# Attention weights times v on one core: the first v in five transfers, cast by GpSimd instead of VectorE

## The chip, the core and the metric

The kernel runs on one core of a Trainium2 chip. The metric is the device time of one execution in microseconds (us), taken as the median of several runs; smaller is better. A profile of one more execution shows what each engine did and when: TensorE (PE, and PEld for its weight loads), VectorE (DVE), ScalarE (ACT), GpSimd (POOL), SyncE (SP) and the DMA engines.

## What is computed

For 8 x 12 = 96 heads, a 1024 x 1024 matrix of attention weights is multiplied by a 1024 x 64 matrix v, all in float32:

```python
def reference(attn_weights, v):   # (8, 12, 1024, 1024), (8, 12, 1024, 64)
    return np.einsum('bhqs,bhsd->bhqd', attn_weights, v).astype(np.float32)
```

The weights alone are 403 MB, so the kernel is for the most part one long stream of loads.

## The kernel before

The 96 heads are taken four at a time: 24 groups (`NV`), each cut into two units by its rows, so 48 units (`NU`). One partition of the tile holds the rows of one of 4 x 32 row blocks of the four heads. A unit's load brings [128, 16, 1024] weights from HBM into one of two buffers `abf` (unit n uses `abf[n % 2]`) and casts float32 to bfloat16 in the DMA itself: 4 MB written for 8 MB read. The program places every buffer and every semaphore by hand; each engine has its own written-out order, and only semaphores tie them together.

**PE** (lines 188 to 221) does, for each unit: wait for the unit's load; 16 groups g of 4 transposes (L132), which bring the summed dimension onto the partitions, into four PSUM banks in turn, so that group g must wait until group g - 4 has been copied out (L129); in the first unit of a group of heads, wait for v (`s_vr`, L197) and spread it over the partitions by small matmuls with a constant matrix (L147); transpose the previous unit's result back (L159); multiply, 64 matmuls (L174).

**VectorE and ScalarE** share the copies out of PSUM (L256 for the transposed weights: VectorE takes 10 of 16 groups, ScalarE 6), the spread v (L232), the products (L268) and the results (L239). VectorE's order starts with memsets (L303 to L307), then the wait for the first v and its cast (L308, L309), then the units.

**GpSimd** issues the loads. Its order is: loads of units 0 and 1 (L341, L342); five affine_selects that make the constants `ident` and `spread`; then for n = 0, 1, ... the load of unit n + 2 (L372, issued at L319), each behind a wait until VectorE's share of unit n's transposes is done on PE (L371), for that frees the buffer. In some rounds it also issues the load of a later v (L325) and the store of a finished result (L332). All of GpSimd's DMAs go through one queue to the 16 DMA engines.

**v**: the v of two groups of heads is loaded at a time. From the second pair on it comes by GpSimd's queue, cast to bfloat16 in the DMA. The first pair is loaded by SP's queue as float32 (L384 to L387) into `v32`, which is the memory of the last two slots of the output buffer, free at that time, and is cast by an engine into `vr`, a [128, 2, 8, 512] bfloat16 tile: 4096 elements a partition. The two halves of `v32` (index `two`) hold one group of heads each. The four transfers are pieces of (half, first partition, number of partitions), a row of 8 KB for each partition; each piece counts 16 on `s_v0`.

**SP** issues these four transfers first, then follows the loads: it tells PE when a unit's load is there (L393 to L396). In one unit (n = 33) it issues 15 tiny transfers of 1 to 15 rows into `small`, which nothing reads (L399 to L402). At the end it issues the last stores (L414 to L421).

The lines around the change: on VectorE, the last two of

```python
for h in range(2):
    nc.vector.memset(ot[:, :, ds(h * HP, HP)], 0.0).then_inc(s_ot[h])
nc.vector.wait_ge(s_v0, 16 * 4)
nc.vector.tensor_copy(out=vr.rearrange("p two b x -> p (two b x)"), in_=v32).then_inc(s_vr, 2)
```

and on PE, the wait of the first unit of each group of heads, which stands behind all of that unit's transposes: `pe.wait_ge(s_vr, it)`.

Of the kernel before, what the change touches and what calls it, by code (L numbers as in the profile page):

```python
# [10 lines left out]
def kernel(  # L11
# [18 lines left out]
    nc = tc.nc  # L30
# [7 lines left out]
    P = 128  # L38
# [4 lines left out]
    HP = P // 2  # L43
# [11 lines left out]
    LOOPED = HELD_FROM  # L55
    NO = 8 + 2
    SMALL_AT = (33,)

    HALVED = NU - 2

    def slot(q):
        return q % 4 if q < LOOPED + 2 else q - LOOPED + 2
# [20 lines left out]
    with tc.tile_critical(no_gpsimd_drain=True):  # L83
# [6 lines left out]
        vr = sb("vr", [P, 2, VB, SB * D], bf16)  # L90
# [4 lines left out]
        v32 = osb[:, ds(NO - 2, 2)].rearrange("p n r d -> p (n r d)")  # L95
# [9 lines left out]
        s_v0, s_v = sem("s_v0"), sem("s_v")  # L105
# [14 lines left out]
        s_memset, s_const, s_vr = sem("s_memset"), sem("s_const"), sem("s_vr")  # L120
# [184 lines left out]

        for h in range(2):
            nc.vector.memset(ot[:, :, ds(h * HP, HP)], 0.0).then_inc(s_ot[h])  # L307
        nc.vector.wait_ge(s_v0, 16 * 4)  # L308
        nc.vector.tensor_copy(out=vr.rearrange("p two b x -> p (two b x)"), in_=v32).then_inc(s_vr, 2)  # L309
        engine(True)  # L310
        engine(False)

# [1 line left out]
        pool = nc.gpsimd  # L314

        def load_attn(n):
            pieces = [(0, G)] if n < HALVED else [(0, GH), (GH, GH)]
            for g0, gn in pieces:
                pool.dma_start(  # L319
                    out=abf[n % 2][:, ds(g0, gn)].rearrange("p g s -> p (g s)"),  # L320
                    in_=attn_q[n // 2][:, ds((n % 2 * G + g0) * S, gn * S)],
                ).then_inc(s_abf[n % 2] if g0 == 0 else s_second[n], 16)

        def load_v(iv):
            pool.dma_start(  # L325
                out=vr.rearrange("p two b x -> p two (b x)"), in_=v_2[iv]
            ).then_inc(s_v, 16)

        def store(q, fours, eng, done):
            eng.wait_ge(s_out, 2 * (q + fours) + 1)  # L330
            at_slot = osb[:, ds(slot(q), fours)].rearrange("p n r d -> p n (r d)")
            eng.dma_start(  # L332
                out=out_2[q // 2] if fours == 2 else out_q[q],
                in_=at_slot if fours == 2 else at_slot[:, 0],
                **({"single_packet": True} if eng is pool else {}),
            ).then_inc(done, 16)

        def store_2(q):
            store(q, 2, pool, s_osb[q // 2 % 2] if q < HELD_FROM else s_held)
# [5 lines left out]
            out=ident,  # L345
            in_=ident,
# [7 lines left out]
        for h in range(VH):  # L354
            pool.wait_ge(s_const, h + 1)
            pool.affine_select(  # L356
                out=spread[ds(h * VP, VP)],
                in_=spread[ds(h * VP, VP)],
# [6 lines left out]
        for n in range(NU - 2):  # L365
            q, i = n // 2, n % 2
            if i == 0 and q % 2 == 1 and q + 1 < NV:
                for s in s_sp:
                    pool.wait_ge(s, 2 * q + 2)
                load_v((q + 1) // 2)  # L370
            pool.wait_ge(s_t[True], (n + 1) * PER_DVE)  # L371
            load_attn(n + 2)  # L372
            if i == 0 and q % 2 == 0 and 0 < q <= HELD_FROM:
                store_2(q - 2)
        for q in range(HELD_FROM, BY_SYNC, 2):
# [5 lines left out]


        v32_2 = v32.rearrange("p (two x) -> p two x", two=2)
        for two, p0, pn in ((0, 0, P), (1, 0, 96), (1, 96, 22), (1, 118, 10)):  # L384
            nc.sync.dma_start(
                out=v32_2[ds(p0, pn), two], in_=v_2[0][ds(p0, pn), two]
            ).then_inc(s_v0, 16)  # L387
        nc.sync.sem_inc(s_free, 2)
        nc.sync.wait_ge(s_const, 1 + VH)
        for n in range(-2, NU - 2):  # L390
# [5 lines left out]
            nc.sync.sem_inc(s_half)  # L396
            if n in SMALL_AT:

                for k in range(1, 16):  # L399
                    nc.sync.dma_start(  # L400
                        out=small[0:k, SMALL_AT.index(n), k, 0 : k + 1], in_=ident[0:k, 0 : k + 1]
                    ).then_inc(s_small, 16)  # L402
# [8 lines left out]
        for k in range(2):  # L411
            nc.sync.wait_ge(s_osb[k], 16 * (HELD_FROM // 4))
        nc.sync.wait_ge(s_small, 16 * 15 * len(SMALL_AT))
        store(NV - 4, 2, nc.sync, s_end)  # L414
        store(NV - 2, 1, nc.sync, s_end)
        for k in range(2):
# [3 lines left out]
            out=out_q[NV - 1], in_=osb[:, slot(NV - 1)].rearrange("p r d -> p (r d)")  # L420
# [33 lines left out]
```

## Time and profile before

| What | Before |
|---|---|
| Median of 3 runs | 1054.7 us (1054.67 to 1054.78) |
| The profiled execution's own time | 1054.48 us |
| Its span, first to last instruction | 1052.7 us |
| Mean granted TensorE clock | 0.867 |
| Busy: PE, DVE, ACT, POOL | 70%, 37%, 38%, 4% of the span |
| Moved by DMA | 240.21 MB, mean 228 GB/s |
| Cast of the first v on VectorE (L309) | once, 2294 ns, begun at 30.75 us |
| Load of a unit, issue to landing (median) | 33.4 us |

How to read the lines that follow. In the page's slices the span is cut into 40 equal parts, and each digit is a busy share in tenths. The chain of waits is followed back from the last instruction to whatever released each step; its pieces show a start, a duration and what ran. A line of the timeline has the start and the duration in us, the engine, the line of the program, the operation, output <- input with its shape, how many instructions were merged, and in brackets the idle time ahead of it and what ended that. Beside these views the trace holds records of every DMA packet (start, duration, size) and of every count that a DMA engine adds to a semaphore when its part of a transfer has landed; "landing" below is the time of such a record, and a load has 16 of them, one for each DMA engine.

### The profile page before, as it was taken

To read this page: it belongs to the slowest core of one execution; us is meant where nothing else is said; L and a number is where in the kernel's file an instruction comes from. 1 tells how busy PE (TensorE), PEld (TensorE's weight loads), DVE (VectorE), ACT (ScalarE), POOL (GpSimd) and SP (SyncE) were. 2 spreads that over 40 slices of the span, in tenths; PEclk is the share of its full clock that TensorE was granted. 3 is DMA by queue.
4 is the path that set the end of the run, shared out by engine and by line. 5 is a ranking of instruction groups with operands and counts; after the bars stand their busy time and mean duration, and the time that the engine had idled before them with its cause. 6 is when DMAs were issued, how large, how long until landed. Compare 5 with 4: busy or idle time off the path is not lost.

```text
span 1052.7 us, 16298 instructions
## 1 busy us (share of the span) xinstructions
PE 732.3 (70%) x6920; PEld 686.6 (65%) x6920; DVE 388.3 (37%) x582; ACT 397.6 (38%) x485; POOL 45.0 (4%) x80
## 2 busy tenths in 40 slices
PE   0777677676687677657768667776766865975885
PEld 0767676566687567656668557765666865864874
DVE  0543343333353234333335324433333433532543
ACT  0443344433353334333335324433333533533543
POOL 1000000000000000000000000000000000000000
PEclk9989888898798888888879878888887987988998
DMA  9999999999999999999999999999999999999998
GB/s 236 223 219 213 210 255 219 219 209 251 225 214 257 219 219 259 215 217 223 238 224 219 258 218 218 254 214 214 246 232 217 219 206 226 217 211 219 216 217 344
DMA packets 14030, 240.21 MB, mean 228 GB/s; under 512 B 1479, under 2 KB 1479, under 8 KB 4295
## 3 DMA queue, kind: packets, MB, share of 16 engines
q0 software_dynamic: 12912, 233.84, 99.1%
q1 hardware_dynamic: 1111, 6.30, 1.5%
q8 instruction: 2, 0.03, 0.0%
q14 instruction: 5, 0.04, 0.0%
HBM read 427.82 MB, written 25.17 MB: 430 GB/s over the span
## 4 chain that ended last, share of the span: by engine, by line
DMA 78%; PE 20%; issue 1%; POOL 0%; DVE 0%; ACT 0%; POOLq 0%; SPq 0%
DMA abf<-in_attn_weights_dram 78%; PE bank L132 20%; PE bank L174 0%; PE bank L159 0%; POOL abf L319 0%; DVE osb L239 0%; ACT ot L268 0%; POOLq L449 0%; SPq L396 0%; SPq L83 0%
## 5 line engine op out<-in xcount | busy, mean ns | idle before, releaser
L132 PE MATMUL bank<-ident,abf 128*128 128x128 f32 x3072 | 448.4, 316 | 277.4 <-DMA abf<-in_attn_weights_dram 272.3
L132 PEld LDWEIGHTS bank<-ident,abf 128*128 128x128 f32 x3072 | 438.5, 214 | 290.7 <-DMA abf<-in_attn_weights_dram 284.4
L256 DVE COPY at<-bank 128x1024 bf16<-128x1024 bf16 x480 | 319.9, 689 | 464.8 <-PE bank L132 463.1
L256 ACT COPY at<-bank 128x1024 bf16<-128x1024 bf16 x288 | 288.7, 1012 | 428.7 <-PE bank L132 428.7
L174 PE MATMUL bank<-at,vbf 128*64 128x256 bf16 x3072 | 215.0, 278 | 0.0
L174 PEld LDWEIGHTS bank<-at,vbf 128*64 128x64 bf16 x3072 | 196.7, 108 | 13.4 <-DVE at L256 4.0
L268 ACT COPY ot<-bank 128x512 f32<-128x512 f32 x48 | 28.1, 585 | 181.0 <-PE bank L174 181.0
L268 DVE COPY ot<-bank 128x512 f32<-128x512 f32 x48 | 33.2, 692 | 151.4 <-PE bank L174 151.4
L159 PE MATMUL bank<-ident,ot 128*128 128x128 f32 x392 | 52.2, 276 | 32.9 <-DVE vbf L232 32.2
L159 PEld LDWEIGHTS bank<-ident,ot 128*128 128x128 f32 x392 | 43.4, 141 | 45.0 <-DVE vbf L232 44.0
L239 ACT COPY osb<-bank 128x512 f32<-128x512 f32 x97 | 52.1, 589 | 22.5 <-PE bank L159 22.5
L319 POOL DMA_DIRECT2D abf<-in_attn_weights_dram x50 | 27.2, 545 | 689.2 <-PE bank L132 688.2
L232 DVE CAST vbf<-bank 128x512 bf16<-128x512 f32 x48 | 30.9, 686 | 6.6 <-PE bank L147 6.6
L232 ACT CAST vbf<-bank 128x512 bf16<-128x512 f32 x48 | 25.8, 589 | 11.9 <-PE bank L147 11.9
L147 PE MATMUL bank<-vr,spread 32*128 32x512 bf16 x384 | 25.8, 377 | 0.0
L325 POOL DMA_DIRECT2D vr<-in_v_dram x11 | 7.7, 704 | 239.7 <-PE bank L147 239.7
L147 PEld LDWEIGHTS bank<-vr,spread 32*128 32x128 bf16 x384 | 10.1, 92 | 6.8
L309 DVE CAST vr<-osb 128x4096 bf16<-128x4096 f32 x1 | 2.3, 2294 | 28.2 <-DMA osb<-in_v_dram 28.2
L332 POOL DMA_DIRECT2D out_dram<-osb x10 | 7.1, 715 | 28.6 <-ACT osb L239 28.6
L256 ACT ACT_TABLE_LOAD x4 | 5.1, 1283 | 1.1 <-SPq L83 1.1
L356 POOL TENSOR_SCALAR_AFFINE_SELECT spread<-spread 32x512 bf16<-32x512 bf16 x4 | 2.5, 629 | 0.6
L239 DVE COPY osb<-bank 128x512 f32<-128x512 f32 x1 | 0.7, 691 | 3.1 <-PE bank L159 3.1
(8 smaller groups left out, 2.1 us busy)
## 6 DMA issues: line engine op xcount, KB each, us to landing
abf<-in_attn_weights_dram POOLq DMA_DIRECT2D x46, 4096.0 KB, 33.4
out_dram<-osb POOLq DMA_DIRECT2D x10, 2048.0 KB, 29.7
vr<-in_v_dram POOLq DMA_DIRECT2D x11, 1024.0 KB, 17.4
abf<-in_attn_weights_dram POOLq DMA_DIRECT2D x4, 2048.0 KB, 24.2
out_dram<-osb SPq DMA_DIRECT2D x1, 2048.0 KB, 14.3
out_dram<-osb SPq DMA_DIRECT2D x2, 1024.0 KB, 12.0
osb<-in_v_dram SPq DMA_DIRECT2D x1, 1024.0 KB
osb<-in_v_dram SPq DMA_DIRECT2D x1, 768.0 KB
```

What stands on the lines that cost most here:

```text
L132: last = pe.matmul(out=pt[g % 4][:, k], lhsT=words[:, k], rhs=ident, is_transpose=True, start=(k == 0), stop=(k == KW - 1),)
L147: last = pe.matmul(out=ps, lhsT=spread[rows, b], rhs=vr[rows, two, b], start=(b == 0), stop=(b == VB - 1),)
L159: last = pe.matmul(out=ps[:, ds(j * P, P)], lhsT=ot[:, j0 + j], rhs=ident, is_transpose=True, start=(j == 0), stop=(j == jn - 1),)
L174: last = pe.matmul(out=outs, lhsT=vbf[:, 2 * kw + par, h], rhs=at[:, ds(half * GH, GH), kw, ds(h * VP, VP), par], start=(n == 0), stop=(n ...
L232: copy(out=vbf[:, :, h], in_=ps.rearrange("p (k d) -> p k d", k=SB)).then_inc(s_vbf[e])
L239: return copy(out=rows.rearrange("p (half j) d -> p j half d", half=2)[:, ds(j0, jn)], in_=ps[:, ds(0, jn * P)].rearrange("p (j half d) -> ...
L256: ins = copy(out=at[:, g].rearrange("c k j two -> c (k j two)"), in_=bank[g % 4].bitcast(bf16),)
L268: copy(out=ot.rearrange("c j (h p) -> c h j p", h=VH)[:, ds(2 * e, 2)], in_=po[e].rearrange("c (h j p) -> c h j p", h=2, j=GH),).then_inc( ...
L319: pool.dma_start(out=abf[n % 2][:, ds(g0, gn)].rearrange("p g s -> p (g s)"), in_=attn_q[n // 2][:, ds((n % 2 * G + g0) * S, gn * S)],).th ...
L325: pool.dma_start(out=vr.rearrange("p two b x -> p two (b x)"), in_=v_2[iv]).then_inc(s_v, 16)
L332: eng.dma_start(out=out_2[q // 2] if fours == 2 else out_q[q], in_=at_slot if fours == 2 else at_slot[:, 0], **({"single_packet": True} if ...
L356: pool.affine_select(out=spread[ds(h * VP, VP)], in_=spread[ds(h * VP, VP)], compare_op=mybir.AluOpType.not_equal, fill=1.0, base=0, patte ...
```

## The change

Three edits. The wait and the cast of the first v leave VectorE's order. GpSimd does the same wait and cast, directly behind its issue of the load of unit 2 (n = 0 in its loop), ahead of its wait for unit 1's transposes. And the first v is transferred in five pieces, two of 64 rows for the first half and 80, 44 and 4 rows for the second, in place of one of 128 rows and 96, 22 and 10.

```diff
+    FIRST_V = ((0, 0, HP), (0, HP, HP), (1, 0, 80), (1, 80, 44), (1, 124, 4))
...
-        nc.vector.wait_ge(s_v0, 16 * 4)
-        nc.vector.tensor_copy(out=vr.rearrange("p two b x -> p (two b x)"), in_=v32).then_inc(s_vr, 2)
         engine(True)
         engine(False)
...
             pool.wait_ge(s_t[True], (n + 1) * PER_DVE)
             load_attn(n + 2)
+            if n == 0:
+                pool.wait_ge(s_v0, 16 * len(FIRST_V))
+                pool.tensor_copy(
+                    out=vr.rearrange("p two b x -> p (two b x)"), in_=v32
+                ).then_inc(s_vr, 2)
...
-        for two, p0, pn in ((0, 0, P), (1, 0, 96), (1, 96, 22), (1, 118, 10)):
+        for two, p0, pn in FIRST_V:
             nc.sync.dma_start(
                 out=v32_2[ds(p0, pn), two], in_=v_2[0][ds(p0, pn), two]
             ).then_inc(s_v0, 16)
```

(`HP` is 64, `P` is 128.)

## The prediction

> **What bounds the kernel now.** I read the page's slices and queue table first, then its chain of waits, then the timeline of the first 70 us, where all that the change touches lies.
>
> ```profile
> PE 732.3 (70%) x6920; PEld 686.6 (65%) x6920; DVE 388.3 (37%) x582; ACT 397.6 (38%) x485; POOL 45.0 (4%) x80
> DMA  9999999999999999999999999999999999999998
> ...
> q0 software_dynamic: 12912, 233.84, 99.1%
> ...
> DMA 78%; PE 20%; issue 1%; POOL 0%; DVE 0%; ACT 0%; POOLq 0%; SPq 0%
> ```
>
> No compute engine is busy over 70%, while the 16 DMA engines stand at 9 in every slice and the queue of GpSimd's loads alone fills 99.1% of their time. The trace's packet records say it more sharply: from 8 to 1040 us at least 15 packets are in flight at any moment. The chain is DMA for 78% and goes through PE for 20%, but that PE share does not cost: a load is issued long before the DMA engines have finished the one in front of it. The chain's merged pieces around the change:
>
> ```profile
> 2.16 46.22 DMA abf<-in_attn_weights_dram
> 48.38 0.04 issue
> 48.42 8.03 PE bank L132 x64
> 56.45 0.29 issue
> 56.74 29.87 DMA abf<-in_attn_weights_dram
> 86.61 0.04 issue
> ```
>
> The load of unit 3 is issued at 56.74, after unit 1's transposes have emptied its buffer, and lands at 86.61. But unit 2's load, ahead of it in the same queue, lands only at 66.22 (first of 16 engines, by the semaphore records) to 67.25 (last). So 56.74 is 9.5 us early, and loads then land 19.33 us apart (110.79, 130.12), whatever PE does. An edit moves the end only if it changes the rows of one DMA engine, or makes an issue so late that the queue runs dry.
>
> **The start, as it is.**
>
> ```profile
> 1.48 1.24 POOL L319 DMA_DIRECT2D abf<-in_attn_weights_dram  x2 [1.04 <-SPq L83]
> 2.84 0.29 POOL L344 TENSOR_SCALAR_AFFINE_SELECT ident<-ident 128x128 f32<-128x128 f32 x1
> 3.27 2.94 POOL L356 TENSOR_SCALAR_AFFINE_SELECT spread<-spread 32x512 bf16<-32x512 bf16 x4
> ...
> 28.80 3.69 PE L132 MATMUL bank<-ident,abf 128*128 128x128 f32 x16 [28.80 <-DMA abf<-in_attn_weights_dram]
> ...
> 30.75 2.29 DVE L309 CAST vr<-osb 128x4096 bf16<-128x4096 f32 x1 [28.18 <-DMA osb<-in_v_dram]
> ...
> 33.70 6.08 PE L132 MATMUL bank<-ident,abf 128*128 128x128 f32 x48 [1.22 <-DVE at L256]
> ...
> 40.08 0.58 POOL L319 DMA_DIRECT2D abf<-in_attn_weights_dram  x1 [33.87 <-PE bank L132]
> ...
> 56.74 0.53 POOL L319 DMA_DIRECT2D abf<-in_attn_weights_dram  x1 [16.08 <-PE bank L132]
> ```
>
> PE begins unit 0 at 28.80, stops after 16 transposes for 1.22 us because VectorE is still casting v, ends at 39.78, and GpSimd issues unit 2's load at 40.08. Then GpSimd idles 16.08 us.
>
> **Step 1, removed: the cast on VectorE.** Its 2.29 us and PE's stall of 1.22 us go. Next late is PE itself: 28.80 + 3.69 + 6.08 = 38.57, so unit 2's load is issued at about 38.57 + 0.30 = 38.87 in place of 40.08. Worth to the end: nothing, since unit 1's data occupy the DMA engines until 46.69 (first engine) either way. If that cover were gone it would be worth at most these 1.2 us.
>
> **Step 2, added: the cast on GpSimd.** No such row is in the trace. Nearest are the two affine_selects: 287 ns for 128 elements a partition, 628 ns for 512. Their slope is 341 / 384 = 0.89 ns an element, with 0.17 us fixed: 4096 x 0.89 + 0.17 = 3.8 us. Ends: 2.3 us, as VectorE, below; 4096 x 287 / 128 = 9.2 us above, if the small tile's mean held. I take 3.8, because the two rows are of different types and sizes and their fixed part need be paid only once. The wait that comes with it should be past: v's last row now lands at 30.66, engines with one row more wait about one 32 KB packet and one row longer (2.43 + 0.32 us), so 33.4, and the cast starts no earlier than 38.87 + 0.58 = 39.45. Queued behind it on GpSimd is the load of unit 3 alone, which waits for PE until 56.74.
>
> **Step 3, moved: everything behind v.** Spreading v starts at 39.72 now and at 39.45 + 3.8 = 43.3 then. From there to unit 0's last product takes 47.63 - 39.72 = 7.91 us now. PE will have idled 4.7 us by then, and after such a gap it is slower: 64 transposes take 9.35 us after the idle 5.57 us before 67.30, and 8.02 us after the idle 0.79 us before 48.42. I add that 1.33 us (a cost of 0 to 1.4 is possible): 43.3 + 7.9 + 1.3 = 52.5. Unit 1's data are there at 48.4, so its transposes start 4.1 us late; they end at 60.5, and unit 3's load is issued at about 60.8 instead of 56.74. VectorE and ScalarE have nothing else to do between, so nothing else is delayed.
>
> **Is 60.8 early enough?** The only delay from a GpSimd issue to its first packet on idle engines that the trace shows is at the start: issued at 1.48, first 32 KB packet at 5.63, 4.15 us. (By the instruction's own 0.53 us it would be less: the other end.) Unit 2's data end about 0.3 us before their landing. The last engine therefore goes idle only if the issue comes after 67.25 - 0.3 - 4.15 = 62.8; the first engine after about 61.5, and its idling alone does not move the end, since it runs 1.0 us ahead of the last. Spare: 2.0 us, that is, a GpSimd cast of up to 5.8 us is free. By the short latency it could be 9.4 us.
>
> **Step 4, the pieces.** 53 landing writes of v are in the records: 16, 16, 11 and 10 for pieces of 128, 96, 22 and 10 rows. So rows a DMA engine now: 8 + 6 on all, 2 more on eleven, 1 more on ten: ten engines with 17, one with 16, five with 14 (sum 256). Read on, 44 rows go to eleven engines by 4 and 4 rows to four by 1: 4 + 4 + 5 on all, then four engines with 18, seven with 17, five with 13 (sum 256). The Trainium skill, DMA: Bandwidth & Descriptors, section on why a DMA increments its semaphore by 16, states that as many engines are used as divide the rows, 16 at most, the lowest-numbered ones; by that the split is the same, and the landing writes agree. A row's packet takes 0.31 to 0.32 us. As the engines are never idle, each keeps this for the whole run: -0.32 us on five, +0.32 on five, 0 on six. Which is last at the end? Landings of the final load run from 1029.77 to 1031.40, and the two last stand apart (1031.34, 1031.40; the next 1031.19). The fifteen small transfers at 785 us, of 1 to 15 rows, load the low-numbered engines most; across them the middle engines of the order fell back by up to 0.18 us and the last two by only 0.06 to 0.08. So the last are more likely among the high-numbered ones, where a row is taken away; but once they gain, others are 0.1 to 0.2 us behind. I take -0.1 us, with bounds of -0.32 and +0.32. A fifth issue on SP (418 ns, the median of the four) ends by 3.5 us, and SP next waits for the constants of GpSimd until 6.2: hidden. The first issue took 714 ns against 384 for the least; a smaller first piece may start the queue up to 0.33 us sooner. I count 0.
>
> **Sum.** The profiled execution: span 1052.7, 1054.48 with what lies around it, 0.2 below the median of 1054.7. 0 + 0 + 0 - 0.1: 1054.6 for the median, no change that matters. About 0.2% (2.1 us) is what a measurement of this kernel can tell from no change.
>
> **Rivals.**
> *The queue runs dry (slower).* Place: unit 3's load, behind PE, behind the GpSimd cast. Point: an issue after 62.8, so a cast above 5.8 us. For it: GpSimd's rate is extrapolated eightfold, and the 4.15 us before the first packet contain 3.5 us that no instruction of GpSimd accounts for, so a first use may cost such a time. With 9.2 us the issue is at 66.2 and all engines idle 3.4 us: 1058.0. With 3.8 + 3.5 = 7.3 it is at 64.3: 1.5 us, 1056.1. With both, 69.7: 6.9 us, 1061.5. Against it: both affine_selects start their work at once. The Trainium skill, GPSIMD Engine Reference, section Instruction dispatch, says that the first call of a freshly loaded kernel on GpSimd waits about 6 us for its code; an estimate by that figure would be 3.8 + 6 = 9.8 us and 1058.6. No row here shows such a wait before an affine_select. Chance 0.22 in all, 0.15 of it beyond 0.2%.
> *The row split decides, with the other sign.* If the last engine is one of the five that gain a row: +0.32, 1055.0. Chance 0.15, all of it within 0.2%.
> *A real gain.* If the loads' start, not the bytes, set the end, the 1.2 us of the removed stall would come through, 1053.5; over 2.1 us would need more than any row shows. Chance 0.05, 0.03 beyond 0.2%.
> *The change does not free VectorE.* If VectorE then waits elsewhere for v, unit 0 stays at 39.78 and the issue of unit 3 moves to 62.0, still before 62.8: no change of time; counted in the forecast.
>
> The forecast has 0.58. Range: from -0.32 and -0.33 together, 1054.0, to the upper bound of the cast, 1058.0. Faster 0.03, within 0.2% 0.82, slower 0.15.
>
> **What would show it.** VectorE's first work is a copy near 29.9, with no gap in unit 0's transposes (step 1). The cast stands on GpSimd near 39.5 with 3.8 us and no wait for v (2). Spreading starts near 43.3, unit 1's transposes near 52.5, the issue at 60.8 (3). Unit 2's landing stays within 0.4 us of 67.25 and unit 3's of 86.61; a later unit 3 alone, with all that follows shifted alike, is the dry queue. Landing writes of v number 63 (4). I am wrong if the cast takes over 6 us, or if GpSimd's issue reaches the engines later than 4.15 us.

## The result and the profile after

The changed kernel takes 1063.2 us (median of 6 runs, 1062.67 to 1063.78), against 1054.74 for the kernel before in the same series: a ratio of 1.0079 with a 95% interval of 1.0068 to 1.0090, so about 8.5 us or 0.8% slower. The forecast of 1054.6 and its whole range, up to 1058.0, missed it. The profiled execution took 1063.17, with a span of 1061.1. (In the profile after, the program's lines are one to five higher or lower than before: L133 is PE's transposes, L148 the spreading of v, L175 the products, L318 the issue of a unit's load, L374 the new cast.)

The lines of the page that answer to those shown of before:

```profile
PE 736.7 (69%) x6920; PEld 690.5 (65%) x6920; DVE 386.1 (36%) x581; ACT 398.0 (38%) x485; POOL 48.6 (5%) x81
...
DMA  9979999999999999999999999999999999999998
...
q0 software_dynamic: 12912, 233.84, 98.4%
...
DMA 76%; PE 22%; issue 1%; POOL 0%; SPq 0%; DVE 0%; ACT 0%; POOLq 0%
```

The third of the 40 slices shows a 7 where before had a 9. Most of the loss lies there: a slice is 26.5 us, and two to three tenths of it are 5 to 8 us in which the DMA engines did nothing. Compute is nearly the same, but for the new cast on POOL. The table of stretches puts the hole between 65 and 75 us; behind the stretch and its length stand the busy times of PE, PEld, VectorE, ScalarE and GpSimd, and the last three columns are the granted clock, the DMA engines' busy share and GB/s; first for the kernel after, then for the kernel before:

```profile
65.00:75.00 10.00, 10.00 (x102) 9.77 (x102) 6.09 (x10) 6.91 (x8) 0.53 (x1) 1.00 0.33 54
```

```profile
65.00:75.00 10.00, 7.71 (x52) 7.71 (x53) 4.65 (x7) 4.26 (x5) 0.00 (x0) 0.72 0.97 210
```

The DMA share falls from 0.97 to 0.33, while PE is busy without a break. By the packet records no data packet starts from 64.9 to 73.2 us on the loads' queue, and the 16 DMA engines stand idle for 6.9 us on average. Why PE was so late is in the chain, here its pieces from 0 to 130 us:

```profile
3.39 45.93 DMA osb<-in_v_dram
49.36 0.10 issue
49.46 3.60 POOL vr L374
53.06 0.56 issue
53.62 1.90 PE bank L148 x15
...
58.85 4.89 PE bank L175 x64
63.74 7.96 PE bank L133 x64
71.70 0.29 issue
71.99 22.50 DMA abf<-in_attn_weights_dram
```

In the chain before, v did not appear at all. Here it leads: the first v lands at 49.3 us instead of 30.7, the cast follows at once, spreading and unit 0's products follow the cast, and only then may PE transpose unit 1, whose data have been there since 49.1. So the load of unit 3 is issued at 71.99, after the DMA engines have finished unit 2 (last landing 67.60). The timeline shows the wait on GpSimd itself:

```profile
27.02 10.32 PE L133 MATMUL bank<-ident,abf 128*128 128x128 f32 x64 [27.02 <-DMA abf<-in_attn_weights_dram]
...
37.64 0.57 POOL L318 DMA_DIRECT2D abf<-in_attn_weights_dram  x1 [31.45 <-PE bank L133]
49.46 3.59 POOL L374 CAST vr<-osb 128x4096 bf16<-128x4096 f32 x1 [11.25 <-DMA osb<-in_v_dram]
53.62 2.13 PE L148 MATMUL bank<-vr,spread 32*128 32x512 bf16 x16 [16.28 <-POOL vr L374]
```

PE's stall in unit 0 is gone, as meant, and the cast takes 3.59 us. But GpSimd idles 11.25 us in front of it, and PE 16.28 us behind it. Comparing the landings of each load with those of before tells when the time is lost: unit 2 on the mean of the 16 DMA engines +0.06 us, unit 3 +7.73, the last load +8.23 (+8.41 on its last engine). Nearly all of it arises at once.

**The theory** ("turns"). While the loads run, a DMA engine takes from the two queues, SP's with v and GpSimd's with the loads, in turn: one 32 KB packet of a load (2.43 us), then one item of v's queue. Such an item is a row of v (0.32 us) or a landing write, one for each piece. So v's landing time is a count of items, not of bytes. It matters how many rows go ahead before the loads begin, and how many pieces there are. The packet records of the changed kernel show such turns: behind the rows of the first piece, v's rows start in sets of 16, as many as there are DMA engines, the first of each set at 6.85, 9.58, 12.31 and 15.04 us, then the 16 landing writes of the second piece from 17.77, then rows again from 20.18. So a row's turn is 2.73 us, and a landing write's 2.41. **Rivals:** the uneven rows of the DMA engines (18, 17, 13) make v late ("split"), or the cast on GpSimd costs the time ("place").

### The profile page after: what moved, and what is told of

It is laid out like the page before. It is cut to its first block, busy times and chain, and to the rows that moved or that the text cites. A ratio compares the mean times of both kernels' runs of the same rounds, so it can differ in the third digit from the quotient of the medians.

```text
span 1061.1 us, 16299 instructions
## 1 busy us (share of the span) xinstructions
PE 736.7 (69%) x6920; PEld 690.5 (65%) x6920; DVE 386.1 (36%) x581; ACT 398.0 (38%) x485; POOL 48.6 (5%) x81
## 4 chain that ended last, share of the span: by engine, by line
DMA 76%; PE 22%; issue 1%; POOL 0%; SPq 0%; DVE 0%; ACT 0%; POOLq 0%
DMA abf<-in_attn_weights_dram 72%; PE bank L133 20%; DMA osb<-in_v_dram 4%; PE bank L175 1%; PE bank L160 0%; POOL vr L374 0%; SPq L389 0%; PE bank L148 0%; DVE vbf L233 0%; DVE osb L240 0%; ACT ot L269 0%; POOL abf L318 0%; SPq L453 0%; SPq L400 0%; POOLq L373 0%
## 5 line engine op out<-in xcount | busy, mean ns | idle before, releaser
L133 PE MATMUL bank<-ident,abf 128*128 128x128 f32 x3072 | 450.4, 317 | 266.7 <-DMA abf<-in_attn_weights_dram 262.4
L133 PEld LDWEIGHTS bank<-ident,abf 128*128 128x128 f32 x3072 | 440.9, 214 | 279.4 <-DMA abf<-in_attn_weights_dram 274.0
L175 PE MATMUL bank<-at,vbf 128*64 128x256 bf16 x3072 | 215.5, 278 | 0.0
L175 PEld LDWEIGHTS bank<-at,vbf 128*64 128x64 bf16 x3072 | 197.1, 108 | 13.7 <-issue 4.2
L318 POOL DMA_DIRECT2D abf<-in_attn_weights_dram x50 | 27.2, 545 | 694.0 <-PE bank L133 693.0
L233 DVE CAST vbf<-bank 128x512 bf16<-128x512 f32 x48 | 30.9, 686 | 23.8 <-PE bank L148 23.8
L148 PE MATMUL bank<-vr,spread 32*128 32x512 bf16 x384 | 26.8, 387 | 16.3 <-POOL vr L374 16.3
L148 PEld LDWEIGHTS bank<-vr,spread 32*128 32x128 bf16 x384 | 10.5, 94 | 23.3 <-issue 16.5
L374 POOL CAST vr<-osb 128x4096 bf16<-128x4096 f32 x1 | 3.6, 3592 | 11.2 <-DMA osb<-in_v_dram 11.2
```

The source lines that it names most:

```text
L133: last = pe.matmul(out=pt[g % 4][:, k], lhsT=words[:, k], rhs=ident, is_transpose=True, start=(k == 0), stop=(k == KW - 1),)
L148: last = pe.matmul(out=ps, lhsT=spread[rows, b], rhs=vr[rows, two, b], start=(b == 0), stop=(b == VB - 1),)
L175: last = pe.matmul(out=outs, lhsT=vbf[:, 2 * kw + par, h], rhs=at[:, ds(half * GH, GH), kw, ds(h * VP, VP), par], start=(n == 0), stop=(n ...
L233: copy(out=vbf[:, :, h], in_=ps.rearrange("p (k d) -> p k d", k=SB)).then_inc(s_vbf[e])
L318: pool.dma_start(out=abf[n % 2][:, ds(g0, gn)].rearrange("p g s -> p (g s)"), in_=attn_q[n // 2][:, ds((n % 2 * G + g0) * S, gn * S)],).th ...
L374: pool.tensor_copy(out=vr.rearrange("p two b x -> p (two b x)"), in_=v32).then_inc(s_vr, 2)
```

## The experiments

The first two take the change apart, the next two test the pieces.

**The cast moved, the pieces left** (`e1_move_only`):

```diff
-    FIRST_V = ((0, 0, HP), (0, HP, HP), (1, 0, 80), (1, 80, 44), (1, 124, 4))
+    FIRST_V = ((0, 0, P), (1, 0, 96), (1, 96, 22), (1, 118, 10))
```

> The pieces of the kernel before (128, 96, 22, 10 rows), the cast on GpSimd as in the change. Theory 'turns' (v lands late because of its pieces, and GpSimd's cast as such is free): v's last landing stays at 30.7 us, the cast runs from about 39 to 42.6, the load of unit 3 is issued near 61, the DMA queue never runs dry, 1054.7 us within 0.5. Theory 'place' (the move of the cast to GpSimd costs the time): at least 4 of the 8.5 us stay, 1059 to 1063.

Measured: 1055.46 us, ratio 1.0003 (0.9994 to 1.0013), no difference. v's last landing is at 30.9. GpSimd's timeline in this kernel:

```profile
39.85 0.57 POOL L318 DMA_DIRECT2D abf<-in_attn_weights_dram  x1 [33.64 <-PE bank L133]
40.47 3.59 POOL L374 CAST vr<-osb 128x4096 bf16<-128x4096 f32 x1
63.52 0.53 POOL L318 DMA_DIRECT2D abf<-in_attn_weights_dram  x1 [19.46 <-PE bank L133]
```

The cast has no wait in front of it, and unit 3's load, though 6.8 us later than before, is early enough. It is 2.5 us later than I had expected (61): 1.5 us because unit 0's transposes began and ran later, so that the cast ended at 44.06, and the rest because PE's work behind the cast was slower after 5.09 us of idling (the spreading took 1.99 us and the products 5.47, against 1.07 and 4.48 before). "Place" is out.

**The pieces changed, the cast left on VectorE** (`e2_pieces_only`), which is the kernel before with

```diff
-        for two, p0, pn in ((0, 0, P), (1, 0, 96), (1, 96, 22), (1, 118, 10)):
+        for two, p0, pn in ((0, 0, HP), (0, HP, HP), (1, 0, 80), (1, 80, 44), (1, 124, 4)):
```

and the wait raised to 16 * 5.

> The five new pieces, the cast on VectorE as before. Theory 'turns': v's last landing is at about 49.3 us as in the changed kernel; VectorE casts to 51.7, unit 0's transposes then need 6.8 more us, the load of unit 2 is issued near 58.8 and moves from 60.0, 11 to 12 us after the DMA engines have finished unit 1 (about 48.5): 1066 to 1068 us. Theory 'place': 1054.7 us within 1.

Measured: 1071.18 us, ratio 1.0149 (1.0132 to 1.0165), 3 us more than expected. The landing, 49.4, is as expected; from its timeline:

```profile
27.34 3.69 PE L132 MATMUL bank<-ident,abf 128*128 128x128 f32 x16 [27.34 <-DMA abf<-in_attn_weights_dram]
...
49.53 2.29 DVE L309 CAST vr<-osb 128x4096 bf16<-128x4096 f32 x1 [46.96 <-DMA osb<-in_v_dram]
...
52.48 8.57 PE L132 MATMUL bank<-ident,abf 128*128 128x128 f32 x48 [21.44 <-DVE at L256]
...
61.35 0.57 POOL L319 DMA_DIRECT2D abf<-in_attn_weights_dram  x1 [55.13 <-PE bank L132]
```

Here VectorE stands in front of v, so unit 0's transposes stop after 16 for 21.44 us, and the load of unit 2, not of unit 3, comes too late. I had given the 48 remaining transposes the 6.1 us of before; after the long idle they took 8.57. So the pieces alone cost 16 us, and moving the cast to GpSimd takes back about half of that, because it lets unit 0's transposes go on.

**The same split of rows, the first half in one piece** (`e3_first_128`):

```diff
+    FIRST_V = ((0, 0, P), (1, 0, 80), (1, 80, 44), (1, 124, 4))
```

> Pieces of 128, 80, 44 and 4 rows: the same 18, 17 and 13 rows a DMA engine as in the change, but the first half of v in one piece. Theory 'turns': v's last landing at about 33.4 us (11 rows and landing writes that wait for a packet of the loads, where before has 10 and the change 18), nothing runs dry, 1054.7 us within 0.5. Theory 'split' (the uneven rows of the DMA engines make v late): the last landing stays near 49 us and the time near 1063.

Measured: 1055.67 us, ratio 1.0002 (0.9992 to 1.0011); last landing 33.5, as counted; unit 3's load at 61.78. The split of 18, 17 and 13 rows is the same as in the change, and the loss is gone. "Split" is out as the cause.

**Even rows, more pieces** (`e4_eight_32`):

```diff
+    FIRST_V = tuple((two, p, 32) for two in range(2) for p in range(0, P, 32))
```

> Eight pieces of 32 rows: 16 rows on each DMA engine, eight landing writes, the cast on GpSimd. Theory 'turns' (each row and each landing write waits for one packet of the loads): 18 to 21 such waits, v's last landing at 53 to 60 us, the load of unit 3 issued 4 to 11 us later than in the changed kernel, 1067 to 1074 us. Theory 'rows alone count': 14 waits, last landing near 42 us, 1054.7 to 1056 us. Theory 'split': even rows, 1054.7 us.

Measured: 1063.80 us, ratio 1.0080 (1.0063 to 1.0097); last landing 49.2. Both numbers fell below what "turns" had given, and far above its rivals. The records show why: 64 rows, two whole pieces, went ahead of the loads' first packet, so 12 rows and 6 landing writes were left, 18 items. The changed kernel has 18 as well, 14 rows on its fullest engines and 4 writes, and lands at 49.3. My mistake was the time of an item, which I had not yet set by the changed kernel itself. With even rows but the same count of items, this kernel loses the same 8.6 us as the changed one.

**What goes ahead, and what a landing write costs.** Four more kernels set the terms of the count apart. Each differs from the changed kernel only in `FIRST_V`, with 16 rows on each DMA engine: 128 and four of 32 (`e8_128_four_32`), 64, 64 and 128 (`e9_64_64_128`), two of 128 (`e5_two_128`), and 96, 32 and 128 (`e11_96_32_128`).

> Pieces of 128 and four of 32 rows, 16 rows on each DMA engine, cast on GpSimd. A first piece of 128 rows lets 10 rows an engine go ahead of the loads; 6 rows and 4 landing writes remain. If a landing write takes a turn like a row: 10 waits, last landing at about 30.7 us. If only rows take turns: 6 waits, about 21 us. Time in either case about 1055.

> Pieces of 64, 64 and 128 rows, 16 rows on each DMA engine, cast on GpSimd. If the length of the first piece sets how many rows go ahead of the loads (4 an engine instead of 10): 12 rows and 2 landing writes wait, last landing at 38 to 42 us. If 10 rows go ahead whatever the pieces are: 6 rows and 2 writes, about 25 us. Unit 3's load is issued before 66 us in either case, time about 1055.

> Two pieces of 128 rows, 16 rows on each DMA engine, cast on GpSimd. 10 rows ahead of the loads, 6 rows and 1 landing write wait: last landing at 22 to 25 us, 6 to 8 us earlier than the 30.4 us of 128 and four of 32 rows, which has three landing writes more. If landing writes cost no turn: 30 us as there. Time about 1055.

> Pieces of 96, 32 and 128 rows, 16 rows on each DMA engine, cast on GpSimd. If the first piece's rows are what goes ahead of the loads: 6 rows an engine, 10 rows and 2 landing writes wait, last landing at 34 to 37 us. If a first piece has to be 128 rows long for any more than 4 to go ahead: 40.6 us, as with 64, 64 and 128. Time about 1055 either way.

Measured, together with the kernels above (rows ahead: rows of v that start before the loads' first packet, from the packet records; items: rows and landing writes left for the fullest DMA engine):

| Pieces | Rows ahead, all engines | Items left | Last landing of v, us |
|---|---|---|---|
| 128, 128 | 160 | 6 + 1 = 7 | 25.1 |
| 128, 96, 22, 10 (before) | 161 | 7 + 3 = 10 | 30.7 |
| 128, 4 x 32 | 160 | 6 + 4 = 10 | 30.4 |
| 128, 80, 44, 4 | 162 | 8 + 3 = 11 | 33.5 |
| 96, 32, 128 | 108 (128, see below) | 8 + 1 = 9 | 29.8 |
| 64, 64, 128 | 64 | 12 + 2 = 14 | 40.6 |
| 64, 64, 80, 44, 4 (after) | 64 | 14 + 4 = 18 | 49.3 |
| 8 x 32 | 64 | 12 + 6 = 18 | 49.2 |

The landing write does take a turn: 128, 128 and 128, 4 x 32 move the same rows, the second leaves three more writes of 4 bytes, and they land 5.3 us apart (three turns of 2.41 are 7.2 us, less about one turn that is saved where a load ends, as said below). What goes ahead depends on the first pieces: about 10 rows an engine behind one of 128, 4 behind one of 64. It is not the length of the first piece alone, for 4 rows an engine go ahead in two pieces of 32 as well; what sets the number stays open.

An item costs 2.75 us (2.43 + 0.32; a landing write a little less) as long as the other queue answers with a 32 KB packet: (25.1 - 5.8) / 7 = 2.76 for two of 128, whose loads begin at 5.8. Where one load ends and the next begins, at 26 to 29 and 46 to 49 us, the loads' own landing write of 0.02 us fills their turn, which saves about one item for each end passed: in the changed kernel 32 rows of v, not 16, start between 25.65 and 26.35, and (49.3 - 4.4) / 2.75 = 16.3 for its 18 items.

One landing missed what was expected: 96, 32 and 128 was to land at 34 to 37 and landed at 29.8. The packet records show why. There the loads' first packets start on some DMA engines at 5.38 and on five of them only at 7.45 to 7.52, and by then 128 rows (the last at 7.02) and 32 landing writes (the last at 7.50) have started, with no gap as long as a turn among them: both first pieces went ahead whole. So 8 rows and 1 write were left, 9 items, one of them saved at the end of unit 0's load: 7.45 + 8 x 2.75 = 29.5. (The records do not name the DMA engine of a packet; this is read from the counts.)

The times, one execution each, are 1054.74 (128, four of 32), 1055.78 (64, 64, 128), 1054.84 (two of 128) and 1055.45 (96, 32, 128), beside medians of 1055.0 and 1055.2 for the kernel before.

**Two queues for v** (`e7_two_queues`), the five pieces as they are:

```diff
-        for two, p0, pn in FIRST_V:
+        for two, p0, pn in FIRST_V[::2]:
             nc.sync.dma_start(
...
+        for two, p0, pn in FIRST_V[1::2]:
+            nc.scalar.dma_start(
```

> The changed kernel with the same five pieces, but the second and fourth issued by ScalarE, so that v lies on two queues. Theory 'turns' (each DMA engine serves its queues in turn): two v items for one packet of the loads, 8 to 10 such rounds, v's last landing at 28 to 33 us instead of 49, nothing dry, 1055.2 us within 0.6. If v as a whole has one share of the DMA engines, whatever the queue, the last landing stays near 49 and the time near 1063.

Measured: last landing 30.5 instead of 49.3, with the same pieces, rows and landing writes. Two things differ, though. With two queues 139 rows go ahead of the loads' first packet (at 6.83) instead of 64, which by itself would move the landing a long way: with 11 more by 7.37, 8 rows and 3 writes are left for the fullest DMA engine, and an estimate of the landing by the count for one queue is 6.8 + 10 x 2.75 = 34.3 (one of the 11 items saved at a load's end). The separate turns show in the packet records themselves: 11 rows of ScalarE's queue start from 13.32 to 13.66, each 0.32 us behind one of the 11 rows that SP's queue starts from 13.00 to 13.34, and the loads' packets follow from 13.63: a row of each queue, then a packet.

The time is 1056.44 us, ratio 1.0013 (1.0004 to 1.0023): a part of a per cent above the kernel before, where I had expected none. This is not a dry queue: between 60 and 80 us the DMA engines idle 0.06 us on average. With two queues ahead of them the loads begin later (first packet at 6.83 instead of 5.63), and they stay late: unit 0 lands 1.50 us later than before on the mean of the DMA engines, unit 3 1.49, and the loads near the end about 1 us.

**Only the first half of v waited for** (`e6_half_casts`), the five pieces as they are, late as they are:

```diff
-                pool.wait_ge(s_v0, 16 * len(FIRST_V))
-                pool.tensor_copy(
-                    out=vr.rearrange("p two b x -> p (two b x)"), in_=v32
-                ).then_inc(s_vr, 2)
+                for two, s in enumerate((s_v0, s_v1)):
+                    pool.wait_ge(s, 16 * sum(x[0] == two for x in FIRST_V))
+                    pool.tensor_copy(
+                        out=vr[:, two].rearrange("p b x -> p (b x)"), in_=v32_2[:, two]
+                    ).then_inc(s_vr)
```

> The changed kernel with its five pieces, but the GpSimd cast cut in two: the first half of v is cast when the first two pieces have landed (a semaphore of its own), the second half after all five. Theory 'late issue' (the loss is unit 3's load issued after the queue ran dry, because all of v was waited for): the first half has landed by 18.5 us, its cast of 1.8 us runs from about 38.2 to 40.1, spreading starts near 40.7, unit 3's load is issued near 59, nothing runs dry, 1055.2 us within 0.6. Theory 'late landing costs by itself' (v's rows slow the loads): the time stays near 1063.

Measured: 1055.65 us, ratio 1.0002 (0.9992 to 1.0011). GpSimd's timeline (L376 is the cast here):

```profile
37.16 0.57 POOL L319 DMA_DIRECT2D abf<-in_attn_weights_dram  x1 [30.95 <-PE bank L133]
37.78 1.89 POOL L376 CAST vr<-osb 128x2048 bf16<-128x2048 f32 x1
49.21 1.90 POOL L376 CAST vr<-osb 128x2048 bf16<-128x2048 f32 x1 [9.54 <-DMA osb<-in_v_dram]
58.79 0.53 POOL L319 DMA_DIRECT2D abf<-in_attn_weights_dram  x1 [7.69 <-PE bank L133]
```

The second half lands at 49.2, as late as ever, and is waited for 9.54 us, and it costs nothing, since nobody needs it before unit 2. So the late rows are harmless by themselves; the wait of unit 0 for all of v is the loss.

**A late issue without late v** (`e10_three_casts`), the pieces of `e3_first_128`:

```diff
+                for k in range(3):
+                    pool.tensor_copy(
+                        out=vr.rearrange("p two b x -> p (two b x)"), in_=v32
+                    ).then_inc(s_vr if k == 2 else s_twice, 2)
+                    if k < 2:
+                        pool.wait_ge(s_twice, 2 * k + 2)
```

> The pieces of 128, 80, 44 and 4 rows, with which v is there by 33.5 us, but GpSimd casts all of v three times in a row (a semaphore between the casts, the same values each time). Theory 'late issue': each further cast costs GpSimd 3.6 us and delays unit 3's load alike, from 61.8 to about 69.1; its first packet moves 1.2 us later, at 70.3; the DMA engines idle some 4 us and the first packets after it are 0.7 us longer: 1059 to 1060.5 us. If the loss in the changed kernel came from v's late rows themselves and not from the late issue, the time stays at 1055.

Measured: 1061.34 us, ratio 1.0056 (1.0040 to 1.0073), 0.8 us above the expected band. v has landed by 33.1, unit 3's load is issued late all the same, and the DMA engines idle 5.4 us on average (L375 is the cast here):

```profile
38.31 0.57 POOL L318 DMA_DIRECT2D abf<-in_attn_weights_dram  x1 [32.11 <-PE bank L133]
38.94 11.05 POOL L375 CAST vr<-osb 128x4096 bf16<-128x4096 f32 x3
70.05 0.53 POOL L318 DMA_DIRECT2D abf<-in_attn_weights_dram  x1 [20.05 <-PE bank L133]
```

The kernels with the cast on GpSimd can now be put in one row, by the time at which unit 3's load is issued and the time (as medians) above the kernel before of their own series:

| Kernel | Issue of unit 3's load, us | Time above before, us |
|---|---|---|
| e6_half_casts | 58.79 | 0.5 (interval holds 0) |
| e3_first_128 | 61.78 | 0.5 (interval holds 0) |
| e1_move_only | 63.52 | 0.3 (interval holds 0) |
| e7_two_queues | 64.94 | 1.3 (all loads late, no dry queue) |
| e10_three_casts | 70.05 | 6.3 |
| after | 71.99 | 8.5 |
| e4_eight_32 | 72.28 | 8.6 |

Issue less loss is 63.5 to 63.8 in the last three, whose queue ran dry, whatever made the issue late. Up to 63.5 us lateness costs nothing that can be told from 0. A line through the three would start to cost at about 63.6 and then a microsecond for each; but it is drawn back from 70 us, the intervals of the losses are 1 to 2 us to each side, and no kernel lies between 65 and 70. The queue itself runs dry only from a later issue: at 64.36 (64, 64, 128) and at 64.94 (`e7_two_queues`, whose loads are 1.4 us late) the DMA engines hardly idle, 0.14 and 0.06 us on average. In the last three they idle 5.4, 6.9 and 7.5 us, so 0.9 to 1.6 us of each loss is not idling itself.

## Why the prediction was wrong, point by point

**What bounds the kernel** was right, and of the two ways in which it said that an edit can cost, a DMA engine's rows or a dry queue, the second is the loss: a dry queue behind unit 3's load. (There is a third way, which `e7_two_queues` shows: a later start of all loads. And its 19.33 us from one landing to the next hold for units 4 and 5; between units 3 and 4 lie 24.2, since a later v is loaded there. Nothing hangs on it.)

**Step 1** held: unit 0's transposes run through without a gap. They took 10.32 us rather than 3.69 + 6.08, and started earlier, at 27.02, for the most part because the loads began earlier, with fewer rows of v ahead of them (first packet at 4.43 us instead of 5.63).

**Step 2** is where it failed. The price of the cast was right: 3.59 us against 3.8, and no delay of a first use showed, the cast beginning 0.14 us after v's last landing. What failed is its sentence on the wait, "v's last row now lands at 30.66, engines with one row more wait about one 32 KB packet and one row longer (2.43 + 0.32 us), so 33.4". I moved the landing by the one row that the split adds, and took everything else of v's 30.66 as given. But that time rested on the first piece: with 128 rows, 161 rows went ahead of the loads' first packet; with 64 rows, 64 did. That is 6 rows an engine more to be taken in turns, one more landing write, and the one row: 8 items more than before, and 49.3 us instead of 30.7. The one row alone would have given 33.5, which is just where the piece of 128 with the same split lands (`e3_first_128`). The packet records of before showed both facts, the 161 rows ahead and that a landing write waits for a 32 KB packet (the second piece's last rows start at 14.5, most of its landing writes between 16.4 and 19.6). I had used these records for the landings only, in step 4, and not asked what the order of the pieces does to them.

The Trainium skill, DMA: Bandwidth & Descriptors, section on queues, rings and completion order, states that a DMA engine goes round its queues in turn, a packet of typically 9 to 17 descriptors (single moves of bytes) at a time. The turns agree with this case; that number does not: v's turn was one row of 8 KB, and a landing write was a turn of its own. The same page, in its anatomy of a DMA issued by GpSimd, calls the landing write on trn2 nearly free; here, on SP's queue beside the busy queue of the loads, a landing write's turn was 2.41 us, nearly all of it waiting.

**Step 3** had the right chain, started too late: from the cast's end to unit 3's issue I counted 17.5 us (43.3 to 60.8), and it took 18.9 (53.05 to 71.99). PE began 0.56 us after the cast's end, where I had put nothing, and the spreading, the transposes back and the products took 2.13, 1.97 and 4.96 us, against 1.07, 1.09 and 4.48 before: 2.4 us more, where I had added 1.33.

**Is it early enough?** The limit of 62.8 came near the 63.6 of the line through the three dry kernels, but by two errors against each other, so this is luck. The delay from an issue to its first packet is not the 4.15 us of the start: in the changed kernel it is 73.22 - 71.99 = 1.23, and 1.24 in `e10_three_casts`. With it the last engine would go idle only from 67.25 - 0.3 - 1.23 = 65.7. On the other side, the first packets after the hole took 3.0 to 3.5 us for the most part instead of 2.43, and idleness of the earlier DMA engines seems not to be free as I had put it: the landings moved as much on the mean (+7.73) as on the last engine (+7.88). No run tests that last point by itself.

**Step 4** had the split right, by the landing writes (63, and two records at 3.5 and 3.9 us, too early for a row of the two smallest pieces; before had two such as well), but its -0.1 us is not confirmed: `e3_first_128`, which shows the split without a dry queue, came out at +0.5 us with an interval that holds 0. Its last load's landings spread over 3.5 us instead of 1.6, the mean 0.5 earlier, the last 1.0 later. In the changed kernel the split hardly counts, as after the hole all 16 DMA engines start together at 73.2 to 74.0.

**The rivals.** The dry queue was named, with its place and nearly its point, but tied to a long cast; a late v that delays the cast was dismissed in step 2, so it had neither a price nor a chance there. That the rival's prices of 1.5 to 6.9 us come close to the measured 8.5 is luck, since they stand for a slow cast, and the cast was as fast as forecast. The worst case of v's landing should have been an end of the range, as the cast's was.

Open remains about half a microsecond of the loss, which comes after unit 3 in small steps (+7.73 to +8.23 on the mean by the last load); the other kernels with a dry queue show 0.4 to 0.9 us of the same, and I did not pursue it.

## What to carry to other kernels

When a small transfer shares the DMA engines with a stream of large packets, count its items, not its bytes: here every row and every landing write that had not gone ahead waited for one large packet. Put as much as possible ahead of the stream (a first piece of 128 rows did more than one of 64), and cut it into as few pieces as the use allows; let the first user wait only for the part that it needs. And when a wait is moved to another engine, ask anew when the awaited thing arrives if the same edit touches how it is sent.

## What was not expected of the hardware

A landing write of 4 bytes, 0.02 us by its own record, held back by a whole 32 KB packet (2.43 us) of another queue. The number of rows that go ahead of a second queue, 64, 128 or about 160, which changed with the first pieces alone. And the matmuls after an idle stretch, for which step 3 added 1.33 us: in the changed kernel, after 16.28 us without work on PE, the 16 spreading matmuls took 2.13 us at a granted clock of 0.50; before, with no idle time ahead, 1.07 us at 1.00. The stretches around them in the two kernels, after first (columns as above):

```profile
53.60:55.80 2.20, 2.13 (x16) 0.93 (x16) 0.26 (x1) 0.20 (x1) 0.00 (x0) 0.50 0.90 194
```

```profile
39.70:40.80 1.10, 1.09 (x17) 0.42 (x16) 0.71 (x2) 0.65 (x1) 0.58 (x1) 1.00 0.28 60
```
